# The softmax probabilities of a transformer block's attention are scaled by 1 / sum on GpSimd, not on VectorE

## The chip, the cores and the metric

One Trainium2 chip, of which the kernel uses one core. A core has five engines with instruction queues of their own: TensorE (matrix products; PE in the profile, with its weight loads as PEld), VectorE (DVE), ScalarE (ACT), GpSimd (POOL) and SyncE (SP, which here only issues loads and stores). Each queue runs in order; an instruction waits at the head of its queue until the semaphores it names have been reached. The metric is the time of one execution on the device, in microseconds (us); less is better.

## The reference, cut to what matters

The reference is a small diffusion transformer: two layers over 256 latent and 256 context tokens of width 1024, in float32. Each layer is a feed-forward part, a mixer (a short convolution in layer 0, attention in layer 1) and another feed-forward part, each behind a normalization that is modulated by vectors made from a condition (`mod`). The change is in the attention of layer 1: 8 query heads, 2 key and value heads, head size 128, 256 queries against 512 keys (context and latent tokens together).

```python
def _attend(q, k, v):
    s = jnp.einsum('bqhgd,bkhd->bhgqk', q, k).astype(jnp.float32) * (ATTN_HEAD_DIM ** -0.5)
    p = jax.nn.softmax(s, axis=-1).astype(v.dtype)
    return jnp.einsum('bhgqk,bkhd->bqhgd', p, v)
...
    mod = (jax.nn.silu(c) @ mod_w[i] + mod_b[i]).reshape(bsz, 3, 3, 1, D_MODEL)
```

## The kernel before, in words

The whole network is one program; activations stay in SBUF, and 245 MB of weights stream in from HBM. Products are made in three passes (`mm3`, lines 112 to 118): each float32 operand is split into a rounded high part and the rest (`split`, lines 91 to 93: ScalarE writes the high part, VectorE the difference), and high x high, high x low and low x high are summed in PSUM. So every weight tile costs ScalarE and VectorE work: `load_w` (101) issues a load of 1 MB on SyncE's queue into one of three raw buffers (`wr`, `load_raw`, 86 to 89) and splits it into `wh` and `wl`.

The modulation vectors of later stages are made on VectorE in the gaps: `tick(n)` (173) lets the next n units of a job list be written into the program. A unit (`mod_unit`, 130) multiplies half a raw buffer of `modT` weights by the condition and sums (line 136, the tile is called `junk`); each job takes one of the three `wr` buffers, and one more `modT` load. The raw buffers are therefore shared by weights and jobs, and a load goes out only when the split or the jobs that read its buffer's former contents are done.

Attention (lines 1007 to 1077) goes head by head, in two halves of 128 queries each:

- `scores(hd)`: per half, three matmuls give the scores `psc` (128 x 512, in PSUM); VectorE takes the row maximum `mx` (1016) and makes the bias `nb` (1018); ScalarE writes the exponentials `e` and their row sum `sm` (1024); VectorE takes the reciprocal `r` (1028) and multiplies: `pn = e * r` (1032). The tile `e` has the tag "sg", with three buffers.
- `turn(pn)`: per half, four transposes on TensorE into `pt` (1041), and a split into `pth` (ScalarE) and `ptl` (VectorE).
- `mix(hd, pt)`: twelve matmuls with the values into `pav` (1060), and a split into the output `a`.

The loop makes the scores two heads ahead, turns one head and mixes the one before it:

```python
    for hd in range(HEADS):
        if hd + 2 < HEADS:
            pns[hd + 2] = scores(hd + 2)
        pts[hd] = turn(pns.pop(hd))
        if hd:
            mix(hd - 1, pts.pop(hd - 1))
        tick(2)
```

`psc`, `pt` and `pav` rotate through the same six PSUM buffers, which hold the projection's sums too. After attention comes the output projection (`project`, weights `wo`, sums `py`, line 1081) on the 256 latent tokens, and then the last feed-forward part (`pg`, `pu`), on them too.

The order of instructions on an engine is not that of the Python code: the framework's planner sorts them within each engine when the program is built, by its own estimate of what each takes, and puts in the semaphores. SyncE's loads keep their order.

Of the kernel before, what the change touches and what calls it, by code (L numbers as in the profile page):

```python
# [13 lines left out]
ALU = mybir.AluOpType  # L14
# [25 lines left out]
def hybrid_kernel(ctx: ExitStack, tc: tile.TileContext, a: dict, out: bass.AP):  # L40
    nc = tc.nc
# [12 lines left out]
    def nm(s):  # L54
        uid[0] += 1
        return f"{s}{uid[0]}"

    def psum(s="ps"):
        return psm.tile([P, T2], F32, tag="mm", name=nm(s))
# [52 lines left out]
    def mm3(ps, w, m, first, last, more=False):  # L112
        wh, wl = w
        mh, ml = m
        kw = {"skip_group_check": True} if more else {}
        nc.tensor.matmul(ps, wh, mh, start=first, stop=False, **kw)  # L116
        nc.tensor.matmul(ps, wh, ml, start=False, stop=False, **kw)  # L117
        nc.tensor.matmul(ps, wl, mh, start=False, stop=last, **kw)  # L118
# [148 lines left out]
    def hot(s, dt=F32R):  # L267
        return hop.tile([P, 1024], dt, name=nm(s), tag="hop")
# [439 lines left out]
    for s in range(2):  # L708
# [6 lines left out]
        out=sb1, in0=modb[:, 0, KT : 2 * KT], scalar1=1.0, scalar2=None, op0=ALU.add  # L715
# [96 lines left out]
    for m in range(KT):  # L812
# [4 lines left out]
        for c0, c1 in ((0, S), (S, T2)) if m == 0 else ((0, T2),):  # L817
# [15 lines left out]
            out=d, in0=u, scalar1=convk[:, 1, m : m + 1], scalar2=None, op0=ALU.mult  # L833
# [4 lines left out]
            out=d2[:, :, 1:], in0=u2[:, :, : S - 1], scalar=convk[:, 0, m : m + 1],  # L838
# [3 lines left out]
            out=d2[:, :, : S - 1], in0=u2[:, :, 1:], scalar=convk[:, 2, m : m + 1],  # L842
# [152 lines left out]
    for kv in range(KVH):  # L995
# [7 lines left out]
        out=scq, in0=rq[:, :16], scalar1=float(P) ** -0.5, scalar2=None, op0=ALU.mult  # L1003
# [3 lines left out]
    def scores(hd):  # L1007
        kv = hd // (HEADS // KVH)
        r_ = []
        for qt in range(2):  # L1010
            o = (hd % 2) * S + qt * P
            ps = psum("psc")
            mm3(ps, tuple(t[:, o : o + P] for t in qs[hd // 2]), ks[kv], True, True)
            ci = hd * 2 + qt
            mx = ap.tile([P, 1], F32, name=nm("mx"), tag="mx", bufs=4)
            nc.vector.reduce_max(mx, ps, axis=AX.X)
            nb = ap.tile([P, 1], F32, name=nm("nb"), tag="nb", bufs=4)
            nc.vector.tensor_scalar(
                out=nb, in0=mx, scalar1=scq[:, ci : ci + 1], scalar2=-1.0,
                op0=ALU.mult, op1=ALU.mult,  # L1020
            )
            e = tp.tile([P, T2], F32, name=nm("e"), tag="sg", bufs=3)
            sm = ap.tile([P, 1], F32, name=nm("sm"), tag="smx", bufs=4)
            nc.scalar.activation(
                out=e, in_=ps, func=AF.Exp, scale=scq[:, ci : ci + 1], bias=nb, accum_out=sm
            )
            r = ap.tile([P, 1], F32, name=nm("r"), tag="r", bufs=4)
            nc.vector.reciprocal(r, sm)
            if qt == 0:
                pn2 = hot("pn", F32)  # L1030
            pn = pn2[:, qt * T2 : qt * T2 + T2]
            nc.vector.tensor_scalar(out=pn, in0=e, scalar1=r, scalar2=None, op0=ALU.mult)
            r_.append(pn)
        return r_

# [16 lines left out]
    def mix(hd, pt):  # L1052
# [11 lines left out]
        aos.append((ah, al))  # L1064

    pns, pts = {0: scores(0)}, {}
    v_proj(2)
    v_proj(3)
    pns[1] = scores(1)
# [7 lines that stand above are left out]
# [90 lines left out]
```

## Time and profile before

| | us |
|---|---|
| median of 3 runs | 1614.27 |
| lowest, highest | 1613.15, 1616.92 |
| the profiled execution | 1611.37 |
| its span in the trace | 1609.5 |

A profile shows one execution. A row of a group or of the timeline names the line of the code, the engine, the operation and `output<-inputs` with shapes; the tiles' names stand without their numbers. In a group, "x16 | 7.6, 483 | idle" means 16 instructions, 7.6 us in all, 483 ns each, and then the time in which the engine stood idle just before them, with what ended it. In the timeline the first number is the start in us, the second the duration; neighbours on one engine overlap a little, as one drains while the next begins. In the chain of waits the numbers are shares of the path that ended last. "<-" names what released a wait.

### The profile page before, as it was taken

Reading aid. Unit: us, or ns where it says so; the run is one execution under the profiler, and the core shown is the slowest. Engines: PE = TensorE matmul, PEld = TensorE weight load, DVE = VectorE, ACT = ScalarE, POOL = GpSimd, SP = SyncE. Lnnn points to the kernel's source line nnn. Section 1 sums busy time; section 2 is a strip of 40 time slices with the busy share of each in tenths; the row PEclk is TensorE's granted clock in tenths of the full one; section 3 lists DMA queues with packets and bytes.
Section 4 is the critical chain, followed back from the end, with each engine's and each line's share of the span. In section 5 each row is a group of like instructions: output and inputs, shape, how many; then the busy total and the mean of one; then the engine's idle time right before and its main releaser. Section 6 shows DMA issues by size and latency. Waiting matters only on the chain.

```text
span 1609.5 us, 25613 instructions
## 1 busy us (share of the span) xinstructions
PE 1576.1 (98%) x10566; PEld 1450.1 (90%) x10566; DVE 1332.4 (83%) x2035; ACT 722.2 (45%) x1110; POOL 0.2 (0%) x4
## 2 busy tenths in 40 slices
PE   9999999999999999999999999999999999899999
PEld 6788998999888889899899889889899897789999
DVE  4988778879998889799797999898898789965554
ACT  5532452544322365335255465245254455454443
POOL 0000000000000000000000000000000000000000
PEclk9999999999999999999999999999999999999999
DMA  8456235234565513353433413452432463755453
GB/s 320 162 183 209 80 122 180 90 135 152 177 221 186 180 41 117 132 183 100 168 120 115 154 54 131 172 195 96 156 129 96 180 214 108 270 201 185 169 194 109
DMA packets 38277, 248.77 MB, mean 155 GB/s; under 512 B 5136, under 2 KB 6928, under 8 KB 12304
## 3 DMA queue, kind: packets, MB, share of 16 engines
q1 hardware_dynamic: 35712, 245.38, 43.7%
q10 hardware_dynamic: 2448, 1.76, 0.4%
q8 instruction: 82, 1.34, 0.3%
q14 instruction: 35, 0.29, 0.1%
HBM read 244.77 MB, written 1.05 MB: 153 GB/s over the span
## 4 chain that ended last, share of the span: by engine, by line
PE 82%; DVE 12%; DMA 3%; ACT 2%; issue 1%; DVEq 0%; ACTq 0%; SPq 0%
PE py L117 7%; PE py L116 7%; PE py L118 7%; PE p L116 6%; PE p L118 6%; PE p L117 6%; PE q L118 5%; PE q L116 5%; PE q L117 5%; DVE junk L136 4%; DVE wl L93 3%; PE pg L117 2%; PE pg L118 2%; PE pg L116 2%; PE pu L117 2%; PE pu L118 2%
## 5 line engine op out<-in xcount | busy, mean ns | idle before, releaser
L92 ACT ACTIVATE wh<-wr 128x1024 fp32r<-128x1024 f32 (+2 forms) x274 | 274.4, 1014 | 395.0 <-PE py L117 108.7
L93 DVE TENSOR_TENSOR wl<-wr,wh 128x1024 fp32r<-128x1024 f32 (+2 forms) x274 | 318.2, 1167 | 97.0 <-ACT wh L92 96.4
L136 DVE CUSTOM_DVE_ANT_0 junk<-wr,scbc,modb 128x1024 bf16<-128x1024 f32 x236 | 302.5, 1282 | 39.6 <-DMA wr<-in_modT 37.0
L117 PE MATMUL py<-gl,wh 128*128 128x512 f32 (+1 forms) x746 | 263.2, 353 | 0.0
L116 PE MATMUL py<-gh,wh 128*128 128x512 f32 (+1 forms) x746 | 263.1, 353 | 0.0
L118 PE MATMUL py<-gh,wl 128*128 128x512 f32 (+1 forms) x746 | 262.9, 352 | 0.0
L93 DVE TENSOR_TENSOR wl<-ws,wh 128x1024 fp32r<-128x1024 f32 x112 | 136.8, 1223 | 27.3 <-ACT wh L92 27.0
L118 PEld LDWEIGHTS py<-gh,wl 128*128 128x128 f32 x746 | 141.1, 189 | 19.1
L116 PEld LDWEIGHTS py<-gh,wh 128*128 128x128 f32 x746 | 141.2, 189 | 18.6
L117 PEld LDWEIGHTS py<-gl,wh 128*128 128x128 f32 x746 | 141.2, 189 | 18.0
L92 ACT ACTIVATE wh<-ws 128x1024 fp32r<-128x1024 f32 x112 | 117.8, 1057 | 76.4 <-PE p L117 34.2
L116 PE MATMUL p<-th,wh 128*128 128x256 f32 x448 | 126.8, 283 | 0.0
L117 PE MATMUL p<-tl,wh 128*128 128x256 f32 x448 | 126.8, 283 | 0.0
L118 PE MATMUL p<-th,wl 128*128 128x256 f32 x448 | 126.6, 283 | 0.0
L117 PE MATMUL q<-bl,wh 128*128 128x256 f32 x336 | 95.2, 283 | 0.0
L116 PE MATMUL q<-bh,wh 128*128 128x256 f32 x336 | 95.1, 283 | 0.0
L118 PE MATMUL q<-bh,wl 128*128 128x256 f32 x336 | 95.1, 283 | 0.0
L438 DVE SCALAR_TENSOR_TENSOR x<-py,G,x 128x256 f32<-128x256 f32 x168 | 74.2, 480 | 21.4 <-PE py L118 21.2
L116 PEld LDWEIGHTS p<-th,wh 128*128 128x128 f32 x448 | 86.0, 192 | 0.5 <-ACT sg L584 0.2
L117 PEld LDWEIGHTS p<-tl,wh 128*128 128x128 f32 x448 | 86.0, 192 | 0.3
L118 PEld LDWEIGHTS p<-th,wl 128*128 128x128 f32 x448 | 85.9, 192 | 0.0
L116 PE MATMUL pg<-hh,wh 128*128 128x256 f32 (+1 forms) x240 | 75.8, 316 | 4.6 <-ACT hh L260 4.6
(236 smaller groups left out, 4001.3 us busy)
## 6 DMA issues: line engine op xcount, KB each, us to landing
wr<-in_w SPq DMA_DIRECT2D x88, 1024.0 KB, 4.9
wr<-in_modT SPq DMA_DIRECT2D x67, 1024.0 KB, 4.9
wr<-in_w2b SPq DMA_DIRECT2D x32, 896.0 KB, 4.6
wr<-in_w2a SPq DMA_DIRECT2D x16, 1024.0 KB, 4.9
wr<-in_cw_cx SPq DMA_DIRECT2D x8, 1024.0 KB, 4.9
wr<-in_mod SPq DMA_DIRECT2D x5, 1024.0 KB, 7.4
wr<-in_cw_b SPq DMA_DIRECT2D x4, 1024.0 KB, 4.8
wr<-in_cw_out SPq DMA_DIRECT2D x4, 1024.0 KB, 4.9
```

The source lines that it names most:

```text
L92: nc.scalar.activation(out=hi, in_=src, func=AF.Copy)
L93: nc.vector.tensor_tensor(out=lo, in0=src, in1=hi.bitcast(F32), op=ALU.subtract)
L116: nc.tensor.matmul(ps, wh, mh, start=first, stop=False, **kw)
L117: nc.tensor.matmul(ps, wh, ml, start=False, stop=False, **kw)
L118: nc.tensor.matmul(ps, wl, mh, start=False, stop=last, **kw)
L136: nc.vector.tensor_tensor_reduce(out=junk, in0=raw[:, j * D : j * D + D], in1=scbc[:, v, :], scale=1.0, scalar=modb[:, l, col : col + 1], ...
L438: nc.vector.scalar_tensor_tensor(out=x[:, m, s * S : s * S + S], in0=ps[:, o : o + S], scalar=g[:, m, s : s + 1], in1=x[:, m, s * S : s * ...
```

## The change

One instruction per half head, sixteen in all, is issued to another engine. What it computes is the same.

```diff
@@ -1029,7 +1029,7 @@
             if qt == 0:
                 pn2 = hot("pn", F32)
             pn = pn2[:, qt * T2 : qt * T2 + T2]
-            nc.vector.tensor_scalar(out=pn, in0=e, scalar1=r, scalar2=None, op0=ALU.mult)
+            nc.gpsimd.tensor_scalar(out=pn, in0=e, scalar1=r, scalar2=None, op0=ALU.mult)
             r_.append(pn)
         return r_
```

Since the planner sorts each queue anew, other instructions change places as well: on VectorE, ScalarE and TensorE from the attention to the start of the last feed-forward part. The order of SyncE's loads is the same.

## The prediction

> **What bounds the kernel now.** I read the page first, then the busy time by stretch around attention, then the chain of waits inside it, then the groups and single instructions of VectorE, then the weight loads behind.
>
> ```profile
> span 1609.5 us, 25613 instructions
> PE 1576.1 (98%) x10566; PEld 1450.1 (90%) x10566; DVE 1332.4 (83%) x2035; ACT 722.2 (45%) x1110; POOL 0.2 (0%) x4
> ```
> ```profile
> 1340.00:1376.00 36.00, 28.18 (x170) 23.00 (x169) 36.00 (x92) 20.55 (x48) 0.00 (x0) 0.93 0.36 129
> 1376.00:1384.00 8.00, 6.89 (x50) 6.52 (x49) 6.68 (x13) 3.53 (x6) 0.00 (x0) 0.91 0.25 81
> 1384.00:1412.00 28.00, 23.65 (x187) 22.48 (x185) 27.07 (x46) 14.10 (x22) 0.00 (x0) 0.99 0.94 333
> ...
> 1420.00:1609.00 189.00, 186.39 (x1552) 185.98 (x1550) 100.30 (x134) 79.75 (x109) 0.00 (x0) 1.00 0.49 168
> ```
>
> Over the whole span TensorE looks like the limit. The stretches (length, then busy time of TensorE, its weight loads, VectorE, ScalarE, GpSimd, then granted clock, DMA share, GB/s) say otherwise for attention: from 1340 to 1376 VectorE is busy 36.00 of 36 us, TensorE 28.18, ScalarE 20.55, GpSimd never. From 1384 to 1412, the output projection, VectorE (27.07 of 28) and DMA (0.94) are both near full. From 1420 TensorE alone is.
>
> ```profile
> by line: DVE mx L1016 23.1%; DVE junk L136 18.4%; DVE ptl L93 18.3%; DVE pn L1032 16.7%; DVE nb L1018 4.5%; DVE a L93 3.9%; PE pt L1041 3.1%; DVE r L1028 3.0%; issue 2.4%; DVE vl L93 1.8%; PE pav L118 1.8%; PE pav L117 1.8%; PE pav L116 1.8
> ```
>
> The chain of waits cut to 1340:1376 runs along VectorE for nearly nine tenths, and the multiply that moves (pn, L1032) is 16.7% of it: 6.0 of 36 us. So, unlike most VectorE work in this kernel, it sits where VectorE's queue sets the end.
>
> **What goes.** Sixteen multiplies leave VectorE.
>
> ```profile
> L136 DVE CUSTOM_DVE_ANT_0 junk<-wr,scbc,modb 128x1024 bf16<-128x1024 f32 x12 | 15.3, 1277 | 0.0
> L1024 ACT ACTIVATE e<-psc,nb,scq 128x512 f32<-128x512 f32 x16 | 12.4, 776 | 12.7 <-DVE nb L1018 12.6
> L93 DVE TENSOR_TENSOR ptl<-pt,pth 128x512 fp32r<-128x512 f32 x16 | 10.6, 683 | 0.0
> L1016 DVE TENSOR_REDUCE mx<-psc 128x1 f32<-128x512 f32 x16 | 10.6, 680 | 0.0
> ...
> L92 ACT ACTIVATE pth<-pt 128x512 fp32r<-128x512 f32 x16 | 9.0, 600 | 3.1 <-PE pt L1041 3.1
> ...
> L1032 DVE TENSOR_SCALAR pn<-e,r 128x512 f32<-128x512 f32 x16 | 7.6, 483 | 0.0
> ...
> L93 DVE TENSOR_TENSOR a<-pav,a 128x256 fp32r<-128x256 f32 x8 | 3.4, 420 | 1.3 <-ACT a L92 1.3
> ...
> L1024 ACT ACTIVATION_READ_ACCUMULATOR e<-psc,nb,scq 128x1 f32 x16 | 3.1, 194 | 0.0
> ...
> L92 ACT ACTIVATE a<-pav 128x256 fp32r<-128x256 f32 x8 | 3.0, 381 | 2.8 <-PE pav L118 2.7
> ...
> L93 DVE TENSOR_TENSOR wl<-wr,wh 128x1024 fp32r<-128x1024 f32 x2 | 2.4, 1216 | 0.0
> ```
> ```profile
> 1343.87 0.49 DVE L1032 TENSOR_SCALAR pn<-e,r 128x512 f32<-128x512 f32 x1
> 1344.28 0.16 DVE L1028 RECIPROCAL r<-sm 128x1 f32<-128x1 f32 x1
> 1344.35 0.20 DVE L1018 TENSOR_SCALAR nb<-mx,scq 128x1 f32<-128x1 f32 x1
> 1344.47 0.49 DVE L1032 TENSOR_SCALAR pn<-e,r 128x512 f32<-128x512 f32 x1
> ```
>
> One multiply lasts 483 ns, but neighbours overlap: the next instruction starts 0.41 us later (1343.87 to 1344.28). What the queue gets back is 16 x 0.40 = **6.4 us**. By the same start-to-start reading r costs 0.07 and nb 0.12; I take 0.60 for mx and ptl, 0.34 for a, 1.20 for a junk job and 1.14 for a wl split, each its duration less the 0.08 of overlap seen on pn.
>
> **What comes: sixteen multiplies on GpSimd.** The trace has no GpSimd work but four memsets of one element, so the price is bounded by rows of other engines: below by VectorE's own 0.483 us, above by the longest VectorE row here, junk's 1.277 us for twice the elements. The nearest row by shape on a third engine is ScalarE's exponential, 0.776. I take **1.0 us**, between that and the upper end, and keep both ends. [...]
>
> Is it hidden? Per head VectorE keeps 2 mx, 2 nb, 2 r, 2 ptl and one a: 1.20 + 0.24 + 0.14 + 1.20 + 0.34 = 3.1 us, and nine junk jobs over eight heads add 1.35: 4.5 us. GpSimd needs 2.0, ScalarE 2 x 0.97 (776 ns and the accumulator read's 194) + 2 x 0.60 + 0.38 = 3.5, TensorE 28.18 us of the 36 for some seven and a half heads, 3.8. VectorE stays the longest, with TensorE next: the cover is 2.5 us per head. Scores are made two heads ahead of their transposes, so a probability tile that comes 0.7 us later normally still waits for TensorE. The exponentials go through three buffers (tag "sg"); one is given back when its multiply is done. Exponential 0.97, the wait for r about 1.2 (one junk job), multiply 1.0 and two handovers make some 3.4 us, against the 6.7 us in which three exponentials are used up at 4.5 us a head. What now waits on GpSimd is ScalarE's next exponential (behind it the pth and a splits) and TensorE's transposes (behind them pav and the next scores). Only the last head has no later scores to cover it: I charge **0.4 us** of the 0.7.
>
> **What moves.** The planner sorts VectorE's queue anew. The same nine junk jobs stand in it up to the last a, but earlier: the changed program has, for heads 4 to 6,
>
> ```
> nb4 nb4 junk r4 mx5 r4 mx5 ptl2 ptl2 a1 nb5 nb5 junk r5 junk r5 ptl3 ptl3 a2
> mx6 mx6 nb6 nb6 junk r6 a3 r6 mx7 ptl4 ptl4 nb7 mx7 junk r7 nb7 junk ptl5 r7 ptl5 a4
> ```
>
> Each pair of junk jobs frees a raw-weight buffer, and SyncE's queue, whose order is unchanged, waits for that.
>
> ```profile
> SPq L88 <- DVE mod L136: 33.9, 8, 8.6
> ...
> 1372.00 0.33 SPq L88 DMA_DIRECT2D wr<-in_wo  x1
> 1380.99 0.33 SPq L88 DMA_DIRECT2D wr<-in_wo  x1
> 1384.83 0.33 SPq L88 DMA_DIRECT2D wr<-in_modT  x1
> ...
> 1384.77 1.20 DVE junk L136
> 1386.00 6.94 DMA wr<-in_wo
> 1392.95 0.02 issue
> ...
> 1414.61 0.58 PE pg L117
> ```
>
> So the first two wo loads (1372.00 and 1380.99) go out earlier, into a stretch whose DMA share is only 0.36. The third starts at 1386.00, when a junk job ends, and takes 6.94 us beside another load. In the new queue two more wl splits stand in front of that job: -6.4 + 2 x 1.14 = -4.1, so it ends near 1381.9 and the load lands near 1389 instead of 1392.95, with those two splits already done. VectorE will then stand idle for some of this time, which it did not before: I charge **0.8 us** for saving that DMA does not pass on, bounded by 0 (all loads move with VectorE) and 6.4 (none do).
>
> **Two engines at one memory.** A junk job that starts while a multiply runs may be slowed, or slow it. No row shows GpSimd and VectorE busy together, so the bounds are 0 and, for the three or four places in the queue above where a junk job directly follows r or nb while a multiply is fresh or unfinished, 4 x 1.0 = 4.0 us. The nearest rows are junk's own 1266 to 1285 ns, the same whatever ScalarE and TensorE do; I stay near the low end and charge **0.8 us**.
>
> **The sum.** -6.4 + 0.4 + 0.8 + 0.8 = **-4.4 us**. The profiled execution took 1611.37 us (span 1609.5 and 1.9 around it), so 1607.0 for its like; it lies 2.9 under the median of 1614.27, which gives **1609.9 us** as median. From 1420 on TensorE is busy 186.39 of 189 us with DMA at 0.49, so what is ahead there stays ahead.
>
> **Rivals.** *GpSimd is much slower than I take it (slower).* In the kernel before, the first r is done at 1338.5 and the last multiply at 1372.4.
>
> ```profile
> 1338.26 0.22 DVE L1028 RECIPROCAL r<-sm 128x1 f32<-128x1 f32 x2
> 1338.39 1.27 DVE L136 CUSTOM_DVE_ANT_0 junk<-wr,scbc,modb 128x1024 bf16<-128x1024 f32 x1
> ...
> 1371.89 0.48 DVE L1032 TENSOR_SCALAR pn<-e,r 128x512 f32<-128x512 f32 x1
> ```
>
> Sixteen multiplies in a row fill these 33.9 us at 2.1 us each. From there GpSimd sets the pace, through the transposes and the three exponential buffers, and each 0.1 us more costs 1.6 us: at 2.6 us it is 8 us, 1622. Against: that is over four times VectorE's row. For: nothing in the trace caps it. 18%.
>
> *VectorE and GpSimd exclude each other (no change).* The queue has four such meetings; if each costs VectorE a whole multiply, 4.0 us replace the 0.8: -4.4 + 3.2 = -1.2, 1613.1. For: the profile before has no overlap to speak against it. Against: in most meetings GpSimd, which has slack, would be the one to wait. 17%. [...]
>
> *The loads hide the gain (no change).* If the projection's loads do not start earlier, everything waits at DMA (0.94) as before: 1614.3. Against: SyncE's waits name VectorE's junk jobs. 7%.
>
> That the multiplies stay on VectorE is ruled out: GpSimd's queue in the changed program holds all sixteen.
>
> **How the numbers follow.** Forecast 58%, with its own range from -7.0 (no charge, and half of VectorE's 1.3 us of idle time in 1376:1384 gone too) to -1.8: 1607.3 to 1612.5. What a measurement can tell from no change is 0.2%, 3.2 us: faster means under 1611.0. The forecast gives 0.52 of its 0.58 to faster, the exclusion rival 0.04: 0.56. No change: 0.06 + 0.12 + 0.07 = 0.25. Slower: the first rival and 0.01 of the second, 0.19. The range 1607.0 to 1617.0 leaves out about 0.15 above (GpSimd over 2.3 us) and 0.03 below.
>
> **What would show it.** Right: VectorE's 36.00 us for the same work shrinks by 5 to 6; GpSimd shows sixteen multiplies near 1 us; exponentials do not wait for GpSimd; the second wo load is issued about 10 us earlier, near 1370, the third near 1382; and the start of the last feed-forward part, 1414 before, moves by 4 us. The exclusion shows as junk at over 1.5 us, or multiplies at 2 us beside junk jobs. Wrong altogether: transposes or exponentials waiting for pn in every head, with VectorE idle.

## The result, and the profile after

| | median us | lowest, highest | runs |
|---|---|---|---|
| before | 1614.62 | 1611.56, 1620.25 | 20 |
| after | 1608.5 | 1605.87, 1613.77 | 20 |

The ratio is 0.9963, with a 95% interval of 0.9953 to 0.9973: 6.1 us less (4.4 to 7.6). The forecast was 4.4 less, 1609.9. The profiled execution of the changed kernel took 1608.07 us.

The head of the page after, and its busy time by stretch in the columns of before (length, TensorE, its weight loads, VectorE, ScalarE, GpSimd, granted clock, DMA share, GB/s):

```profile
span 1606.2 us, 25631 instructions
PE 1577.2 (98%) x10566; PEld 1450.9 (90%) x10566; DVE 1326.2 (83%) x2019; ACT 722.3 (45%) x1110; POOL 29.7 (2%) x20
```
```profile
1340.00:1376.00 36.00, 29.39 (x180) 24.50 (x180) 33.63 (x85) 21.86 (x52) 28.40 (x16) 0.95 0.46 150
1376.00:1384.00 8.00, 8.00 (x68) 7.89 (x67) 7.75 (x13) 5.46 (x9) 1.12 (x1) 1.00 0.37 128
1384.00:1412.00 28.00, 23.89 (x184) 22.88 (x183) 27.30 (x50) 13.62 (x22) 0.00 (x0) 0.93 0.93 346
```

VectorE's 36.00 of 36 us has become 33.63: it now has idle time in this stretch. GpSimd is busy 28.40 us in it, and 1.12 in the next, with sixteen multiplies, far from the 16 that sixteen of 1.0 us would make. The groups of the attention stretch, and the list of the tile pn (least, median and longest ns):

```profile
L1032 POOL TENSOR_SCALAR pn<-e,r 128x512 f32<-128x512 f32 x16 | 29.5, 1858 | 1347.2 <-DVE r L1028 1345.2 <-PE pt L1041 1.4 <-DVE nb L1018 0.6
L136 DVE CUSTOM_DVE_ANT_0 junk<-wr,scbc,modb 128x1024 bf16<-128x1024 f32 x12 | 15.3, 1275 | 0.0
L1024 ACT ACTIVATE e<-psc,nb,scq 128x512 f32<-128x512 f32 x16 | 12.4, 777 | 10.1 <-DVE nb L1018 8.5 <-POOL pn L1032 0.9 <-DVE ptl L93 0.8
...
L1041 PE MATMUL pt<-ident,pn 128*128 128x128 f32 x64 | 9.9, 286 | 4.4 <-POOL pn L1032 3.0 <-DVE ptl L93 1.4
```
```profile
L1032 POOL TENSOR_SCALAR pn<-e,r x16: 1559/1566/2633, 1341.5 to 1375.6; 128x512 f32<-128x512 f32 x16
```

An undisturbed multiply takes 1.566 us on GpSimd, the longest 2.633. Yet the exponentials waited only 0.9 us for it in all, and the transposes 3.0 (the weight loads ahead of them, 5.4; these run beside other matmuls, busy for 1450.9 of the 1606.2 us in which matmuls are busy for 1577.2). VectorE's junk took 1275 ns, against 1277 before. (Of the 1345.2 us of idle time, 1341.05 are GpSimd's wait from the start of the program to its first multiply.)

The chain of waits from 1340 to 1376 is no longer VectorE's alone:

```profile
by line: POOL pn L1032 15.6%; DVE junk L136 12.6%; DVE mx L1016 11.9%; PE pt L1041 9.7%; DVE ptl L93 8.3%; PE pav L117 6.6%; PE pav L116 5.9%; PE pav L118 5.8%; issue 5.6%; ACT e L1024 4.5%; PE psc L116 2.5%; PE psc L117 2.5%; DVE nb L1018 
```

The multiply has gone from 16.7% of this stretch on VectorE to 15.6% on GpSimd, so it is still on the path in places, though VectorE's queue is rid of it. The end of attention moved all the same. Three points of the program place the gain: the first mx (L1016), the last a, and the first t (L250) of the last feed-forward part.

```profile
1333.80 0.68 DVE L1016 TENSOR_REDUCE mx<-psc 128x1 f32<-128x512 f32 x1
...
1383.22 0.42 DVE L93 TENSOR_TENSOR a<-pav,a 128x256 fp32r<-128x256 f32 x1
...
1411.76 0.48 DVE L250 SCALAR_TENSOR_TENSOR t<-x,A,ss 128x256 f32<-128x256 f32 x1
```

These are VectorE's rows of before in order of time; the next three are the same of after.

```profile
1336.68 0.68 DVE L1016 TENSOR_REDUCE mx<-psc 128x1 f32<-128x512 f32 x1
...
1382.53 0.42 DVE L93 TENSOR_TENSOR a<-pav,a 128x256 fp32r<-128x256 f32 x1
...
1409.84 0.48 DVE L250 SCALAR_TENSOR_TENSOR t<-x,A,ss 128x256 f32<-128x256 f32 x1 [0.20 <-PE ss L242]
```

The first mx comes 2.9 us later in this execution of the changed kernel, although the change touches nothing ahead of it; so points are compared from the first mx on. Two more profiles of each kernel were taken later (below), and show how far one execution can be trusted:

| us | before, three profiles | after, three profiles | difference of means |
|---|---|---|---|
| first mx to last a | 49.42, 48.74, 49.93 | 45.85, 45.97, 46.00 | -3.4 |
| first mx to first t (L250) | 77.96, 77.86, 79.18 | 73.16, 74.45, 73.46 | -4.6 |
| first t to the end | 197.74, 197.14, 197.80 | 196.36, 197.41, 196.40 | -0.8 |

Some 4.6 of the 6.1 us lie in attention and projection. The 0.8 behind them is no more than three profiles of one kernel differ by; the rest is not placed. These profiles can't place it: the six executions themselves lie only 4.45 us apart in the mean (1612.08 and 1607.63).

What kind of time the 4.6 us are, the busy times from the first mx to the first t tell (columns as above; before, then after):

```profile
1333.80:1411.76 77.96, 64.92 (x452) 58.06 (x450) 75.70 (x163) 41.97 (x83) 0.00 (x0) 0.96 0.55 194
```
```profile
1336.68:1409.84 73.16, 63.51 (x452) 57.64 (x450) 69.83 (x146) 41.78 (x83) 29.52 (x16) 0.96 0.60 208
```

VectorE does the same work but for the sixteen multiplies (one instruction at the edges counts in or out), and it is nearly always busy, through the projection too. In the mean of three profiles it is busy 75.80 us before and 69.88 after, 5.9 less, and idle 2.5 and 3.8, 1.3 more: 5.9 - 1.3 = 4.6. The same two numbers stand below with the experiments that bear on it.

### The profile page after: what moved, and what is told of

The parts are those of the page before. It is cut to its first block, busy times and chain, and to the rows that moved or that the text cites. A ratio compares the mean times of both kernels' runs of the same rounds, so it can differ in the third digit from the quotient of the medians.

```text
span 1606.2 us, 25631 instructions
## 1 busy us (share of the span) xinstructions
PE 1577.2 (98%) x10566; PEld 1450.9 (90%) x10566; DVE 1326.2 (83%) x2019; ACT 722.3 (45%) x1110; POOL 29.7 (2%) x20
## 4 chain that ended last, share of the span: by engine, by line
PE 86%; DVE 9%; DMA 2%; ACT 1%; issue 1%; POOL 0%; ACTq 0%; SPq 0%; DVEq 0%; POOLq 0%
PE py L116 8%; PE py L117 8%; PE py L118 8%; PE p L116 7%; PE p L118 7%; PE p L117 7%; PE q L118 5%; PE q L116 5%; PE q L117 5%; DVE junk L136 3%; PE pg L117 2%; PE pg L116 2%; PE pg L118 2%; PE pu L116 2%; PE pu L118 2%; PE pu L117 2%
```

## The experiments

The theory, called Q: VectorE's queue is the limit in attention, and taking 16 x 0.40 us out of it is the gain; where the multiply runs matters only as long as its new engine has slack. Its main rival, called S: the planner sorted all queues anew, and the new order is the gain.

**Half of the multiplies.** The first half of each head stays on VectorE.

```diff
-            nc.gpsimd.tensor_scalar(out=pn, in0=e, scalar1=r, scalar2=None, op0=ALU.mult)
+            eng = nc.gpsimd if qt else nc.vector
+            eng.tensor_scalar(out=pn, in0=e, scalar1=r, scalar2=None, op0=ALU.mult)
```

> The second half (qt = 1) of each head is multiplied on GpSimd, the first half still on VectorE: eight of the sixteen multiplies move. Theory Q (the gain is the time that VectorE's queue gets back): half of it, 2.5 to 3.5 us under the kernel before, ratio near 0.998. Rival S (the gain comes from the new sorting of the queues, with jobs and loads earlier; the freed time itself is not needed): its queue has the late order of the changed kernel, so 5 us or more under before. Rival G (GpSimd's pace costs time, so fewer multiplies there are better): GpSimd never falls behind, so more than half of the gain, 4 to 6 us.

Measured: 1610.14 us against 1614.42, ratio 0.9977 (0.9969 to 0.9986): 3.7 us gained (2.3 to 5.0) with half of the queue time saved. That is near Q and reaches S's 5 us or more only at its edge, but it does not exclude rival G's 4 to 6. From the first mx to the last a there are 47.99 us, between the 49.4 and 45.9 of the two kernels. From the first mx to the first t VectorE is busy 73.25 us, 2.6 less than before and 3.4 more than after, and idle 1.7.

**The multiply on both engines.** GpSimd makes pn, and VectorE does the same work once more into a tile that nobody reads. VectorE's queue has its load back; GpSimd's part and a new order stay.

```diff
             nc.gpsimd.tensor_scalar(out=pn, in0=e, scalar1=r, scalar2=None, op0=ALU.mult)
+            scr = ap.tile([P, T2], F32, name=nm("scr"), tag="scr", bufs=1)
+            nc.vector.tensor_scalar(out=scr, in0=e, scalar1=r, scalar2=None, op0=ALU.mult)
```

> GpSimd multiplies as in the changed kernel, and VectorE does the same multiply again into a tile that nobody reads: VectorE's queue has its 16 x 0.40 = 6.4 us back, GpSimd's latency stays. Theory Q: the gain is gone and GpSimd's latency shows, 0 to 4 us over the kernel before. Rival S: the queue behind attention is sorted as in the changed kernel, so 2 to 6 us under before remain.

Measured: 1616.73 us, ratio 1.0009 (1.0001 to 1.0018). The whole gain is gone, and by the ratio 1.5 us more (0.2 to 2.9). VectorE's groups of this kernel show where these can come from:

```profile
L136 DVE CUSTOM_DVE_ANT_0 junk<-wr,scbc,modb 128x1024 bf16<-128x1024 f32 x12 | 15.7, 1310 | 0.0
L1034 DVE TENSOR_SCALAR scr<-e,r 128x512 f32<-128x512 f32 x16 | 10.1, 632 | 0.0
```

The second multiply takes 632 ns in the mean where VectorE's own took 483: 16 x 0.15 = 2.4 us of delay beside GpSimd. From the first mx to the first t VectorE is busy 78.66 us, 2.9 more than before, and idle 2.8. Of S nothing is left as a main cause. No experiment holds the order fixed, and here it is a third one; but with the same VectorE instructions in this stretch an order can shorten it only through VectorE's idle time, and that is 2.5 us before, 3.8 after and 1.7 and 2.8 in these two kernels, while the busy time follows the multiplies that VectorE is given.

**The multiply left out.** The exponentials go to the transposes unscaled, so the softmax is not divided by its sum; r is still made.

```diff
-            e = tp.tile([P, T2], F32, name=nm("e"), tag="sg", bufs=3)
+            if qt == 0:
+                pn2 = hot("pn", F32)
+            pn = pn2[:, qt * T2 : qt * T2 + T2]
+            e = pn
...
-            nc.gpsimd.tensor_scalar(out=pn, in0=e, scalar1=r, scalar2=None, op0=ALU.mult)
```

> The multiply is left out: the exponentials are written straight into the tile that is transposed, unscaled, and r is made but not used. VectorE has the same 6.4 us back as in the changed kernel, and no latency of a multiply is left on any engine. Theory Q: 6 to 9 us under the kernel before, the surplus over the changed kernel (6.1) being what GpSimd's latency costs it (TensorE waited 3.0 us for pn there). Rival S: behind attention its VectorE queue is sorted like that of the kernel before, so less is gained than with the changed kernel, 2 to 4 us. If GpSimd's latency is all hidden: 6 us as well.

Measured: 1607.96 us, ratio 0.9958 (0.9946 to 0.9969): 6.8 us gained (5.0 to 8.7), where the changed kernel's interval is 4.4 to 7.6. So GpSimd's 1.6 us per multiply cost the whole too little to be told from nothing. Within attention they do cost: from the first mx to the last a there are 42.46 us in the one profile, 6.9 under before and 3.5 under after. But to the first t there are 73.11, with after's mean at 73.69. Of the 3.5 us, 1.1 is a wl split, which stands ahead of the last a in the changed kernel and behind it here. ScalarE's waits around the projection (1376 to 1412) show what takes most of the rest; first of after, then of this kernel:

```profile
ACT wh L92 <- DMA wr<-in_wo: 2.1, 1, 2.1
```
```profile
ACT wh L92 <- DMA wr<-in_wo: 6.1, 2, 5.9
```

ScalarE's splits wait 4.0 us longer for the wo loads than in the changed kernel (before, they wait 8.2 in its first profile), and VectorE stands idle for ScalarE's wh for 2.6 us, 0.2 in the changed kernel. So what attention gains beyond after's 3.4 us runs mostly into the weights' arrival. To the first t VectorE is busy 69.58 us and idle 3.5, near after's 69.88 and 3.8.

**Each multiply twice on GpSimd.** The same instruction is issued two times over.

```diff
             nc.gpsimd.tensor_scalar(out=pn, in0=e, scalar1=r, scalar2=None, op0=ALU.mult)
+            nc.gpsimd.tensor_scalar(out=pn, in0=e, scalar1=r, scalar2=None, op0=ALU.mult)
```

> Each multiply is issued twice on GpSimd, so that a half head costs 2 x 1.566 = 3.13 us of GpSimd; the order of the other queues is that of the changed kernel. If GpSimd sets the pace from 2.1 us a half head on, as the first rival of the prediction had it: 16 x (3.13 - 2.1) = 16 us over the kernel before, with transposes and exponentials waiting for pn. If GpSimd's time is hidden: as the changed kernel, 6 us under before.

Measured: 1625.97 us, ratio 1.0072 (1.0056 to 1.0089). Its waits (us in total, times, longest) and the busy time from 1340 to 1390:

```profile
ACT e L1024 <- POOL pn L1033: 19.1, 8, 4.1
PE pt L1042 <- POOL pn L1033: 15.7, 10, 2.7
```
```profile
1340.00:1390.00 50.00, 30.92 (x157) 23.55 (x155) 33.51 (x80) 21.28 (x48) 49.35 (x30) 0.85 0.33 116
```

GpSimd is busy 49.35 of 50 us, exponentials wait for it 8 times and transposes 10: the first rival of the prediction, brought about here. Against after it costs 17.5 us, or 1.09 per head half, for 1.566 us more work. If all time past some point costs its full length, GpSimd sets the pace from 1.566 + (1.566 - 1.09) = 2.04 us per half, an estimate from these two kernels. The changed kernel runs 0.5 us per half under that point. The prediction's 2.1 was the point at which the time of before is reached again; this kernel is 11.6 us over before (9.0 to 14.4) in place of the 16 expected, which puts that point at 3.13 - 11.6 / 16 = 2.4.

**The multiply on ScalarE.**

```diff
-            nc.gpsimd.tensor_scalar(out=pn, in0=e, scalar1=r, scalar2=None, op0=ALU.mult)
+            nc.scalar.activation(out=pn, in_=e, func=AF.Identity, scale=r)
```

> The sixteen multiplies go to ScalarE (Identity with the scale r) in place of GpSimd; VectorE's queue loses the same 6.4 us. Theory Q (VectorE's queue time is the gain, and whoever takes the multiply only needs slack): ScalarE was busy 20.55 of the 36 us of attention, 16 more operations of about 0.6 us are 9.6, so it stays under VectorE; 4 to 7 us less than before, ratio 0.9957 to 0.9975. Rival T (a short, even multiply beside VectorE is worth more than GpSimd's 1.6 us one): 7 us or more gained, ratio under 0.9957. Rival A (ScalarE's queue is on the path through pth, a and the exponentials behind the multiply, which waits for r at the head of the queue): under 3 us gained, ratio over 0.998, with exponentials and pth idle behind r.

Measured: 1611.58 us, ratio 0.9981 (0.9972 to 0.9991), 3.1 us gained (1.5 to 4.5), half of what GpSimd brings. That lies at the edge of rival A's bounds, and the interval reaches into Q's: it does not decide between them.

```profile
L1032 ACT ACTIVATE pn<-e,r x16: 709/722/760, 1338.9 to 1374.2; 128x512 f32<-128x512 f32 x16
```
```profile
1340.00:1376.00 36.00, 28.26 (x159) 23.52 (x158) 34.08 (x83) 29.61 (x63) 0.00 (x0) 0.91 0.46 166
```

At 722 ns the operation is less than half as long as GpSimd's, yet worth less: ScalarE is now busy 29.61 of 36 us, and exponentials, pth and a stand in the same in-order queue. TensorE's waits for pth and e appear in the profile, and the chain of 1340 to 1376 names ScalarE first (e 12.7%). The multiplies wait for r only 1.0 us in this stretch, so it is not the wait at the head of the queue that rival A named. The order also took three more wl splits and one more junk job in ahead of the last a (4 and 13, where before has 1 and 12). From the first mx to the first t this one profile shows 79.17 us, no gain at all: VectorE is busy 71.91 us, 3.9 less than before, but idle 7.3, which is 4.7 more; in 3.2 of them it waits for ScalarE's wh. The profiled execution took 1611.94 us, no less than the profiled ones of before, so it can't place the 3.1 us; where they lie is open.

**Spare multiplies beside VectorE.** The kernel before, with 64 more multiplies on GpSimd near the start.

```diff
+    gscr = mp.tile([P, T2], F32, name="gscr", tag="gscr", bufs=1)
+    for _ in range(64): nc.gpsimd.tensor_scalar(out=gscr, in0=scbc[:, 0, :T2], scalar1=modb[:, 0, 0:1], scalar2=None, op0=ALU.mult)
```

> The kernel before, with 64 more multiplies on GpSimd near the start (128x512 from SBUF to SBUF, one scalar per partition, about 42 to 150 us of the span); nobody reads their result. VectorE works there at nearly nine tenths on junk (1283 ns), wl splits, hl and t. One-sided theory (a GpSimd multiply that begins beside a VectorE operation with two SBUF inputs waits for it; the VectorE operation that begins beside a multiply runs on): junk stays within 1270 to 1290 ns, the multiplies spread from 1.55 to over 2.5 us, the total stays within 0.2%. Exclusion theory (the second to start is blocked until the first is done): about 40 of VectorE's longer operations in this stretch grow by up to 1.5 us, junk's mean goes to 1.8 us or more, and the total grows by 10 us or more if VectorE is on the path there. Delay by class (operations with one input or a scalar per partition are delayed by 0.4 us, those with two are not): hl and t (484 and 483 ns) show 0.9 us while wl and junk don't.

Measured: 1621.57 us, ratio 1.0053 (1.0034 to 1.0073), 8.6 us more. All three expectations missed in the main: VectorE is delayed, but by 0.35 and 0.40 us in the rows below and not by a whole multiply of 1.57, and two-input operations too. From the timeline (start, duration):

```profile
102.24 1.57 POOL L806 TENSOR_SCALAR gscr<-scbc,modb 128x512 f32<-128x512 f32 x1
102.39 1.62 DVE L136 CUSTOM_DVE_ANT_0 junk<-wr,scbc,modb 128x1024 bf16<-128x1024 f32 x1
...
110.55 2.14 POOL L806 TENSOR_SCALAR gscr<-scbc,modb 128x512 f32<-128x512 f32 x1
110.66 0.68 DVE L93 TENSOR_TENSOR gl<-gm,gh 128x512 fp32r<-128x512 f32 x1
111.26 1.62 DVE L93 TENSOR_TENSOR wl<-wr,wh 128x1024 fp32r<-128x1024 f32 x1
112.78 2.65 POOL L806 TENSOR_SCALAR gscr<-scbc,modb 128x512 f32<-128x512 f32 x1
112.81 1.27 DVE L136 CUSTOM_DVE_ANT_0 junk<-wr,scbc,modb 128x1024 bf16<-128x1024 f32 x1
```

A junk job that begins 0.15 us after a multiply takes 1.62 us, 0.35 more than its 1.27, and the multiply its undisturbed 1.57. Where junk begins within 0.03 us of the multiply (112.81), junk runs at 1.27 and the multiply takes 2.65, 1.08 more. The gl that begins 0.11 us after the multiply of 110.55 takes 0.68, as in the kernel before (0.69), and the multiply 2.14, 0.57 more; the wl that follows gl at 111.26 takes 1.62, 0.40 more than the 1.22 of before. So in each of these meetings one of the two was longer: the multiply by up to 1.08 us, or VectorE's operation by 0.35 to 0.40. Junk, gl and wl have two inputs in SBUF. No gm, one of whose inputs is pu in PSUM, was longer: at most 680 ns in this stretch, where the kernel before has 680 to 687.

The longest multiply, 2.10 us over its 1.57, lies beside two such operations, of which VectorE begins the second 0.08 us before the first ends:

```profile
155.44 1.21 DVE L93 TENSOR_TENSOR wl<-wr,wh 128x1024 fp32r<-128x1024 f32 x1
155.47 3.67 POOL L806 TENSOR_SCALAR gscr<-scbc,modb 128x512 f32<-128x512 f32 x1
156.57 1.22 DVE L93 TENSOR_TENSOR wl<-wr,wh 128x1024 fp32r<-128x1024 f32 x1
```

**Narrower spare multiplies.** The same with 96 of half the width.

```diff
+    gscr = mp.tile([P, 256], F32, name="gscr", tag="gscr", bufs=1)
+    for _ in range(96): nc.gpsimd.tensor_scalar(out=gscr, in0=scbc[:, 0, :256], scalar1=modb[:, 0, 0:1], scalar2=None, op0=ALU.mult)
```

> The kernel before, with 96 spare multiplies of half the width (128x256) on GpSimd in the same place; nobody reads their result. With 512 elements an undisturbed one took 1.57 us, one that began beside a two-input VectorE operation up to 2.65, and a VectorE operation that began 0.1 to 0.2 us after a multiply took up to 0.40 more. [...] For the price: if a multiply is all per element, 0.78 us; if half of it is a fixed part, 1.2.

The multiplies and the split hl (484 ns in the kernel before) of this kernel, then hl beside the wide ones:

```profile
L806 POOL TENSOR_SCALAR gscr<-scbc,modb x96: 922/1326/3032, 41.4 to 193.7; 128x256 f32<-128x256 f32 x96
...
L261 DVE SCALAR_TENSOR_TENSOR hl<-t,mod,hh x8: 473/686/694, 45.0 to 68.8; 128x256 fp32r<-128x256 f32 x8
```
```profile
L261 DVE SCALAR_TENSOR_TENSOR hl<-t,mod,hh x8: 473/898/930, 46.4 to 72.5; 128x256 fp32r<-128x256 f32 x8
```

The median delay is 0.21 us with 256 elements (686 against the least of 473) and 0.42 with 512 (898 against 473): half the width, half the delay, so one that is the same at both widths is out. Junk reached 1497 ns here and 1620 beside the wide ones, where an undisturbed one takes 1270. The longest multiply took 3.03 us, again beside two operations in a row (a junk job and a wl split). The least of 922 ns against 1565 for twice the width makes 643 / 256 = 2.5 ns per element and a fixed 0.28 us per multiply, an estimate from two widths. A single run took 1618.2 us, beside 1615.68 of before.

**Both kernels again.** Two more profiles of each, unchanged.

> The kernel before, unchanged, for a second profile: from the first mx to the last split of a, to the first t of the last feed-forward part and to the end were 49.42, 77.96 and 275.7 us. If the differences of the changed kernel (3.57, 4.80 and 6.18 less) are its own, this profile repeats each within 0.7 us; if the 1.4 us behind the last feed-forward's start are scatter, its 197.74 us from there to the end change by a like amount.

> The changed kernel, unchanged, for a second profile: 45.85, 73.16 and 269.52 us from the first mx to the same three points, and 196.36 from the last feed-forward's first t to the end. The same readings within 0.7 us if they are its own; otherwise they scatter by the 1 to 1.5 us that the rest behind the last feed-forward's start would need.

> A third profile of the kernel before. From the first mx to the last feed-forward's first t the two so far show 77.96 and 77.86 us, and from there to the end 197.74 and 197.14; the changed kernel's two show 73.14 and 74.49, and 196.36 and 197.41. If 4 us of the gain lie between the first mx and that t and nothing certain behind it, the third gives 77.5 to 78.3, and 196.5 to 198.

> A third profile of the changed kernel: 73 to 74.6 us from the first mx to the last feed-forward's first t, 196.3 to 197.5 from there to the end; less than 72.5 in the first would make it a gain of over 5 us in attention and projection.

They took 1612.23, 1608.93, 1612.65 and 1605.9 us; their intervals stand in the table above. Two of them fall outside what was expected: after's second profile, with its first t at 74.45 in place of 73.16 and its end at 271.9 in place of 269.52, and before's third, at 79.18 in place of 77.5 to 78.3. One profile places a gain in this kernel to about 1 us; the single profile's -4.8 and -1.4 (from the first t on) are therefore given as -4.6 and -0.8, the second within scatter.

## Why the prediction was right, by its steps

**What goes: 6.4 us.** Right, if a little high: from the first mx to the first t VectorE is busy 5.9 us less. Half of it back (3.7 of 6.1 gained) and all of it back (no gain) follow it, and without any multiply attention is 6.9 us shorter.

**GpSimd's multiply at 1.0 us.** Wrong in size: 1.566 us undisturbed and 1.858 in the mean, above the upper bound of 1.277. The bounds were rows of other engines, the upper one an operation of twice the elements, and GpSimd's time lies outside them. The step held because it was not asked for more: the cover, worked out as 2.5 us per head, swallowed most of the error. What the error could have cost, the doubled multiply tells: 0.5 us more per half, and GpSimd would have set the pace.

**The last head: 0.4 us.** Too small, and in the wrong place. It is part of a lateness of 0.7 us that the prediction does not work out; 1.566 in place of 0.483 alone makes 1.1. VectorE's groups between the first mx and the last a of after:

```profile
L1016 DVE TENSOR_REDUCE mx<-psc 128x1 f32<-128x512 f32 x16 | 10.6, 682 | 0.9 <-PE psc L118 0.9
...
L93 DVE TENSOR_TENSOR wl<-wr,wh 128x1024 fp32r<-128x1024 f32 x3 | 3.6, 1214 | 0.0
L93 DVE TENSOR_TENSOR a<-pav,a 128x256 fp32r<-128x256 f32 x8 | 3.3, 416 | 1.0 <-ACT a L92 1.0
...
L1028 DVE RECIPROCAL r<-sm 128x1 f32<-128x1 f32 x16 | 2.3, 156 | 0.7 <-ACT e L1024 0.6
```

The idle time is 2.6 us (0.9 + 1.0 + 0.7) where it was 1.3 (a); in the mean of three profiles 2.7 and 1.3, so 1.4 more. In the first profile 2.4 of the 2.6 us lie 9.5 to 32.5 us behind the first mx, in the earlier heads that the prediction took as covered; behind that only 0.25 are left, where before has its whole 1.3. The account of the first profile is -6.4, +1.1 for a second wl split that now stands ahead of the last a (before has one; the wl group counts one more in each kernel, which begins 0.08 us before that a ends), +1.3 of idle time: -4.0, measured -3.6. Against the kernel without the multiply, attention is 3.5 us longer, of which one wl split is 1.1.

**DMA passes not all of it on: 0.8 us.** Such a loss was seen: the kernel without the multiply gains 3.5 us more in attention and only 0.6 at the first t, with 4.0 us more of waiting for wo than after. In the changed kernel itself the charge was not paid: between the last a and the first t VectorE is idle 1.2 us in the mean of before's profiles and 1.1 in after's. GpSimd's latency and the waits for the weights (DMA share 0.94 before and 0.93 after, from 1384 to 1412) overlap there, and the two charges are not to be added as the sum did. The issues of SyncE's loads after:

```profile
1368.18 6.33 SPq L88 DMA_DIRECT2D wr<-in_wo  x2
...
1385.29 0.33 SPq L88 DMA_DIRECT2D wr<-in_wo  x1
```

The row of two starts at 1368.18 and ends with the second issue, which lasts 0.33: that one is at 1374.2. Counted from the first mx the second wo load goes out at 37.5 us where it was 47.2, 9.7 earlier (predicted about 10). The third is 3.6 earlier (48.6, from 52.2; predicted 4.1). What releases it is the second of two wl splits behind the last a, not a junk job as in the prediction, and it lands at 53.4, from 59.2. The first t moves by 4.6 (predicted 4).

**Two engines at one memory: 0.8 us.** Nothing of this size fell on VectorE: junk's mean is 1275 ns (1277 before). In the changed kernel the multiply is the one that takes longer, as the prediction's argument against that rival said; five of the sixteen take 2.3 to 2.6 us, all begun 0.07 to 0.39 us behind the start of a junk job, and the other eleven 1.56 to 1.57:

```profile
1341.26 1.27 DVE L136 CUSTOM_DVE_ANT_0 junk<-wr,scbc,modb 128x1024 bf16<-128x1024 f32 x1
1341.47 2.49 POOL L1032 TENSOR_SCALAR pn<-e,r 128x512 f32<-128x512 f32 x1 [1341.05 <-DVE r L1028]
...
1355.62 1.56 POOL L1032 TENSOR_SCALAR pn<-e,r 128x512 f32<-128x512 f32 x1
...
1356.50 1.27 DVE L136 CUSTOM_DVE_ANT_0 junk<-wr,scbc,modb 128x1024 bf16<-128x1024 f32 x1
```

The multiply of 1341.47 begins beside a junk job and takes 2.49 us; the junk job of 1356.50 begins 0.9 us into a multiply and takes its usual 1.27, as does the multiply its 1.56. No junk job in this order of work begins less than 0.88 us behind the start of a multiply. Beside the spare multiplies one begun 0.15 us behind was 0.35 us longer, so the charge stands for a delay that exists, but this order of work doesn't meet it. In the kernel with half of the multiplies on VectorE it is paid, by 0.43 us:

```profile
1341.45 1.27 DVE L136 CUSTOM_DVE_ANT_0 junk<-wr,scbc,modb 128x1024 bf16<-128x1024 f32 x1
1341.72 2.43 POOL L1033 TENSOR_SCALAR pn<-e,r 128x512 f32<-128x512 f32 x1 [1341.30 <-DVE r L1028]
1342.64 0.08 DVE L136 DVE_READ_ACCUMULATOR2_ANT mod<- 128x1 f32 x1
1342.64 0.91 DVE L1033 TENSOR_SCALAR pn<-e,r 128x512 f32<-128x512 f32 x1
```

GpSimd's multiply, begun 0.27 us behind junk, takes 2.43 in place of 1.57, and VectorE's own multiply, next behind junk, 0.91 in place of 0.48. Another of VectorE's multiplies in the same kernel, which begins 1.2 us into an undisturbed GpSimd multiply, takes 0.67, and the cause of that smaller delay is open:

```profile
1347.68 1.56 POOL L1033 TENSOR_SCALAR pn<-e,r 128x512 f32<-128x512 f32 x1 [3.53 <-DVE nb L1018]
1348.86 0.67 DVE L1033 TENSOR_SCALAR pn<-e,r 128x512 f32<-128x512 f32 x1
```

**The sum.** -4.4 against -6.1 (-7.6 to -4.4). What bounds the kernel and what the change takes away were right, but that the sum comes so near to the 4.6 us that the profiles place is in part luck. There 6.4 was 5.9, the last head's 0.4 was 1.4 of idle time, spread over attention, and of the two charges of 0.8 nothing was found: the errors cancel. The 1.5 us between 4.6 and 6.1 are not placed. Of the rivals, a slow GpSimd came half way (1.566 us, between the 1.0 taken and the rival's 2.1), the delay of the exclusion rival was there but fell on GpSimd (0.75 to 1.07 us on five multiplies), which had slack (28.40 of 36 us busy), and the loads took a part of the gain only where the multiply was left out.

## What to carry to other kernels

A short operation can be worth moving off the engine whose queue is full even to one that takes three times as long for it, as it was here (1.566 us against 0.483, and 6.1 us gained), where a few tiles of buffer lie between it and its consumer: find the pace at which the new engine takes over (here about 2.04 us per operation) and stay under it. The engine with the shorter operation need not be the better place when its queue holds others on the path (ScalarE, 0.722 us for the operation, brought 3.1 us of the 6.1). Look at what the time saved runs into next: here even leaving the multiply out gained only 6.8 us, and weight loads took a part of what attention saved (4.0 us more of waiting for wo than in the changed kernel). And to tell time saved from a lucky order, add up the full engine's busy and idle time over a stretch with the same work.

## What the runs showed of the hardware that was not expected

- GpSimd's multiply by one scalar per partition, SBUF to SBUF in float32: 1.566 us for 128 x 512 and 0.922 for 128 x 256, the least of 96; an estimate from these two is 2.5 ns per element and 0.28 us fixed. VectorE takes 0.483 for the larger, ScalarE 0.722 (Identity with a scale).
- Where a GpSimd multiply and a VectorE operation with two inputs in SBUF ran beside each other, one of them mostly took longer. The multiply: 2.32 to 2.63 us for 1.57 where it began 0.07 to 0.39 us behind a junk job, 2.65 where junk began 0.03 us behind it, 3.67 beside two wl splits without a gap. VectorE's operation: junk 1.62 for 1.27 where it began 0.15 us behind the multiply, hl in the median 0.90 for 0.47 beside multiplies of 512 elements and 0.69 beside those of 256. A junk job begun 0.88 us behind a multiply took its 1.27.
- VectorE's multiply with one input in SBUF was longer as well: 0.91 for 0.48 right behind a junk job and beside a GpSimd multiply, 0.67 where it began 1.2 us into a GpSimd multiply, 0.632 in the mean of sixteen where both engines multiply. Three operations with an input in PSUM were not: gm stayed at 680 ns or less among 64 spare multiplies, and beside the sixteen of the changed kernel mx took 682 ns and ptl 678, where before has 680 and 683.
